# A two-layer decoder on one core: the gates' high product as scaled copies on ScalarE, late TensorE parts held behind first products, and a new schedule of gather steps

## The chip, the cores and the metric

The kernel runs on one core of one Trainium2 chip. The metric is the device time of one execution in microseconds (us). All tensors come in as float32; products of float32 matrices are made from bfloat16 halves, as told below.

## What is computed

Two layers, each a token mixer (layer 0: a gated linear recurrence beside chunked retention; layer 1: a chunked state-space mixer) and then a mixture of 16384 small experts ("PEER"), with residuals and root-mean-square norms. The change touches the expert mixer alone:

```python
q = (t @ w_q).reshape(n_tok, 8, 2, 64)
scores = einsum('thpk,hpnk->thpn', q, sub_keys)
s_top, i_top = top_k(scores, 16)
cand = s_top[:, :, 0, :, None] + s_top[:, :, 1, None, :]
best, pos = top_k(cand.reshape(n_tok, 8, 256), 16)
expert = take_along_axis(cand_idx, pos); gates = softmax(best)
u = u_emb[expert]
act = gelu(einsum('td,thkd->thk', t, u)) * gates
out = einsum('thk,thkd->td', act, v_emb[expert])
```

There are 512 tokens of width 1024, so four tiles of 128 tokens. Each token has 8 x 16 = 128 experts.

## The kernel before

**Two ways to the experts.** Tile 0 (`GT`) gathers: for its 128 tokens the kernel fetches the chosen rows of `u` and `v` by indirect DMA (`gather`, L785). Tiles 1 to 3 (`DT`, 384 tokens) are computed densely: 128 blocks of 128 experts, each with a *first product* `up(b)` (24 matmuls of 384 columns into `pu`, then a Gelu on ScalarE, L909), a multiplication with the block's gates (L1014) and a second product into six accumulators `acc` (18 matmuls of 512 columns, L82 to L84).

**Split products.** `split` (L75, L76) makes a bfloat16 high half on ScalarE and a low half on VectorE or GpSimd; `mm3` (L82 to L84) adds high x high, high x low and low x high. Weights come through `Stream`: a DMA, `whi` on ScalarE, `wlo` on GpSimd, three tiles ahead.

**The head.** After the mixer's output projection the expert part begins with a head. It routes tile 0 and then tiles 1 to 3 (`routing`: eight scores `ps`, L656, each followed by top-8 searches on VectorE; candidates; index arithmetic with the tiles `eq`, `em`, L714 to L721; then transposes into `pt`, L737 and L755). For each group of 16 tokens `gate_group` builds a dense gate table for all 16384 experts: VectorE compares the iota with the two indices (`o2`, L928; `ol`, L930), multiplies with the gate's high half (`oh`, L932) and its low half (`ol`, L933); TensorE multiplies `o2` with `oh` and `ol` per token into `pg` (L941, L942); ScalarE copies to `st` (L943), and a DMA writes `Gd`. There are 24 groups in a layer. The head is cut into 183 units (`UNITS`); `fill` puts between them first products ahead of time (`RUN[1]` = `AHEAD` + `SPILL` = 95 of 128), and `EARLY` = 100 of the 262 gather steps. First products of blocks below `SPILL` are written to DRAM (`Hd`) and read back.

**Gather steps.** One step starts one gather and uses the one of six steps before: a `u` row block is dotted with the token on VectorE (`junk`, L814), four `v` row blocks are summed in two halves of four matmuls (`av`, L839) with an addition to the residual on VectorE (L843). Steps not taken in the head are taken at the ticks of the blocks, evenly.

**The blocks.** `load_gates` reads `Gd` back (L1003) once the last group is written, and blocks 0 to 127 follow, with the remaining 33 first products between them.

**What sets the order.** The program text gives instructions their rank and buffers; a scheduler turns it into one fixed list per engine when the kernel is built. `tc.issue_after(x)` adds that an instruction stands behind `x` in its engine's list; `due` lists in `fill` say after how many units (`LATE` = 3) a transposition or a group's matmuls are put in.

## Time and profile before

| | us |
|---|---|
| median of 3 runs (lowest, highest) | 3517.67 (3515.95, 3518.49) |
| the profiled execution | 3519.76 |
| its span in the profile | 3518.0 |
| TensorE busy in the span | 3219.2 (92%) |
| VectorE busy | 2313.1 (66%) |
| GpSimd busy | 1932.0 (55%) |
| ScalarE busy | 1443.8 (41%) |

Busy is the time in which an engine has at least one instruction in work; matmuls overlap, and their ends are modelled, so a busy TensorE is not one at its peak. The profiled execution lies 2.1 us above the median, and 1.8 us of it lie outside the span. In layer 0 the head runs from 490.6 to 1042.2 us of the span and the blocks to 1733.0; in layer 1 the head runs from 2267.4 to 2821.8 and the blocks to 3510.2.

### The profile page before, as it was taken

To read this page: it belongs to the slowest core of one execution; us is meant where nothing else is said; L and a number is where in the kernel's file an instruction comes from. 1 tells how busy PE (TensorE), PEld (TensorE's weight loads), DVE (VectorE), ACT (ScalarE), POOL (GpSimd) and SP (SyncE) were. 2 spreads that over 40 slices of the span, in tenths; PEclk is the share of its full clock that TensorE was granted. 3 is DMA by queue.
4 is the path that set the end of the run, shared out by engine and by line. 5 is a ranking of instruction groups with operands and counts; after the bars stand their busy time and mean duration, and the time that the engine had idled before them with its cause. 6 is when DMAs were issued, how large, how long until landed. Compare 5 with 4: busy or idle time off the path is not lost. (4 is left out here: it accounts for less than half of the span.)

```text
span 3518.0 us, 52562 instructions
## 1 busy us (share of the span) xinstructions
PE 3219.2 (92%) x19786; PEld 1730.0 (49%) x19786; DVE 2313.1 (66%) x4286; ACT 1443.8 (41%) x2303; POOL 1932.0 (55%) x1122
## 2 busy tenths in 40 slices
PE   7999977988899999999998888788888999999999
PEld 4444554554554444444455554554545644444444
DVE  6555289977766767433567774889886677675433
ACT  5444443343443333333445555433434433333333
POOL 4444756766656665554233345577666656555552
PEclk9999999999999999999999999898999999999999
DMA  4222657797999999876321124587878999998773
GB/s 142 89 82 86 194 169 251 259 305 251 303 331 345 341 366 335 301 266 229 117 78 61 61 72 124 159 273 243 299 246 285 333 348 359 359 339 289 282 251 120
DMA packets 340672, 821.91 MB, mean 234 GB/s; under 512 B 28353, under 2 KB 179393, under 8 KB 336321
## 3 DMA queue, kind: packets, MB, share of 16 engines
q1 hardware_dynamic: 133632, 456.22, 38.0%
q0 software_dynamic: 73728, 268.47, 21.2%
q10 hardware_dynamic: 133056, 93.87, 8.3%
q8 instruction: 155, 2.54, 0.3%
q14 instruction: 101, 0.82, 0.1%
HBM read 732.98 MB, written 85.46 MB: 233 GB/s over the span
## 5 line engine op out<-in xcount | busy, mean ns | idle before, releaser
L76 POOL TENSOR_TENSOR wlo<-w,whi 128x1024 bf16<-128x1024 f32 x536 | 1199.3, 2240 | 1210.6 <-ACT whi L75 1128.3
L75 ACT ACTIVATE whi<-w 128x1024 bf16<-128x1024 f32 x696 | 730.4, 1051 | 840.2 <-PE pu L83 336.4
L82 PE MATMUL pu<-hh,whi 128*128 128x384 bf16 x2048 | 676.7, 330 | 12.3 <-ACT Hs L909 12.3
L84 PE MATMUL pu<-hh,wlo 128*128 128x384 bf16 x2048 | 675.3, 330 | 0.0
L83 PE MATMUL pu<-hl,whi 128*128 128x384 bf16 x2048 | 675.2, 330 | 0.0
L84 PE MATMUL acc<-whi,al 128*128 128x512 bf16 x1536 | 582.8, 379 | 1.4 <-DVE al L76 1.3
L82 PE MATMUL acc<-whi,ah 128*128 128x512 bf16 x1536 | 583.6, 380 | 0.0
L83 PE MATMUL acc<-wlo,ah 128*128 128x512 bf16 x1536 | 583.0, 380 | 0.0
L76 DVE TENSOR_TENSOR al<-a,ah 128x384 bf16<-128x384 f32 x256 | 154.7, 605 | 492.0 <-ACT ah L75 463.2
L814 DVE CUSTOM_DVE_ANT_0 junk<-g,hr 128x1024 bf16<-128x1024 f32 x256 | 372.2, 1454 | 89.1 <-DMA g<-u_in,ix 82.7
L82 PEld LDWEIGHTS <-whi 128*128 128x128 bf16 x2944 | 290.7, 99 | 228.7 <-issue 48.4
L83 PEld LDWEIGHTS <-whi 128*128 128x128 bf16 x2944 | 290.9, 99 | 208.7 <-issue 27.4
L84 PEld LDWEIGHTS <-wlo 128*128 128x128 bf16 x2944 | 290.7, 99 | 204.0 <-issue 21.2
L785 POOL DMA_INDIRECT g<-v_in,ix x256 | 319.4, 1248 | 126.0 <-PE av L839 68.3
L75 ACT ACTIVATE ah<-a 128x384 bf16<-128x384 f32 x256 | 133.5, 522 | 615.5 <-issue 449.9
L785 POOL DMA_INDIRECT g<-u_in,ix x256 | 323.5, 1264 | 105.7 <-issue 36.8
L82 PEld LDWEIGHTS <-ah 128*128 128x128 bf16 x1536 | 150.2, 98 | 234.7 <-issue 32.6
L84 PEld LDWEIGHTS <-al 128*128 128x128 bf16 x1536 | 150.4, 98 | 185.1 <-DVE al L76 3.1
L83 PEld LDWEIGHTS <-ah 128*128 128x128 bf16 x1536 | 150.4, 98 | 171.1 <-issue 2.4
L76 DVE TENSOR_TENSOR wlo<-w,whi 128x1024 bf16<-128x1024 f32 x160 | 195.6, 1223 | 16.8 <-ACT whi L75 15.4
L1014 DVE TENSOR_TENSOR a<-Hs,G 128x384 f32<-128x384 f32 x168 | 156.8, 935 | 68.3 <-DMA G<-Gd 46.8
L82 PE MATMUL mm<-hhi,whi 128*128 128x512 bf16 x512 | 196.2, 383 | 1.1 <-DVE cv L195 1.1
(384 smaller groups left out, 4913.1 us busy)
## 6 DMA issues: line engine op xcount, KB each, us to landing
w<-ut_in SPq DMA_DIRECT2D x256, 512.0 KB
w<-v_in SPq DMA_DIRECT2D x256, 512.0 KB
Gd<-st ACTq DMA_DIRECT2D x48, 1024.0 KB
G<-Gd SPq DMA_DIRECT2D x32, 1536.0 KB
w<-w_in SPq DMA_DIRECT2D x88, 512.0 KB
w<-wo_in SPq DMA_DIRECT2D x64, 512.0 KB
Hd<-Hs ACTq DMA_DIRECT2D x168, 192.0 KB
Hs<-Hd SPq DMA_DIRECT2D x168, 192.0 KB
```

Of the source, the lines that this page charges most:

```text
L75: nc.scalar.activation(hi, src, AF.Copy)
L76: return (lo_eng or nc.vector).tensor_tensor(lo, src, hi, op=OP.subtract)
L82: nc.tensor.matmul(out, ah, bh, start=start and i == 0, stop=False)
L83: nc.tensor.matmul(out, ah, bl, start=False, stop=False)
L84: nc.tensor.matmul(out, al, bh, start=False, stop=stop and i == n - 1)
L785: nc.gpsimd.indirect_dma_start(out=g, out_offset=None, in_=tab, in_offset=bass.IndirectOffsetOnAxis(ap=ix, axis=0))
L814: nc.vector.tensor_tensor_reduce(k.junk, g, hr, op0=OP.mult, op1=OP.add, scale=1.0, scalar=0.0, accum_out=h[:, s:s + 1])
L1014: nc.vector.tensor_tensor(a.rearrange("p (a b) -> p a b", b=GB), H[b].rearrange("p (a b) -> p a b", b=GB), g, op=OP.mult)
```

## The change

- `gate_group`: the comparison goes into a tile `om` of its own (one buffer). The high product is no longer one multiplication on VectorE but 16 copies on ScalarE, one per token, each of 128 x 128 with the token's gate as a per-partition factor (`gT`, a float32 copy of the transposed gates). The low product stays on VectorE and now reads `om`.
- `behind()`: the transposes of the routing, the groups' matmuls and the first of the four matmuls of each `av` half stand behind the last matmul of the latest first product in TensorE's list.
- `sums` calls `flush()` first, so that a second half still open is put in.
- `WAIT` = 7: gather steps, and the closing transposition of tile 0, begin after 7 units instead of 3.
- `SPILL` 84 to 90 and `AHEAD` 11 to 7: 97 instead of 95 first products in the head, 90 instead of 84 results written to DRAM and read back, 8 instead of 12 buffers for results that stay.
- `EARLY` 100 to 84: 16 gather steps move from each head into the blocks. There, a tick counts 2 below block 90 and 3 from it on (`PACES`).

```diff
-SPILL = 84
-AHEAD = 11
+SPILL = 90
+AHEAD = 7
...
-EARLY = 100
+EARLY = 84
...
+WAIT = 7
...
+PACES = 2, 3
...
+        gT = one.tile([128, TD], F32, name="gT")
...
+        latest = []
+
+        def behind():
+            return tc.issue_after(latest[-1].ins) if latest else nullcontext()
...
-            nc.tensor.transpose(pt[:, 0], e2[:, 1], k.ident)
+            with behind():
+                nc.tensor.transpose(pt[:, 0], e2[:, 1], k.ident)
...
             split(nc, pt[:, 2], ghl[:, 0, ts], ghl[:, 1, ts])
+            nc.scalar.activation(gT[:, ts], pt[:, 2], AF.Copy)
...
             def sums(i, r, h):
 
+                flush()
                 nc.scalar.activation(h, h, AF.Gelu_apprx_tanh)
...
-                            with tc.issue_after(first.ins) if first is not None else nullcontext():
+                            with tc.issue_after(first.ins) if first is not None else behind():
...
-            ticks = KEYS + KEYS - RUN[1] - SLACK
+            ticks = PACES[0] * SPILL + PACES[1] * (KEYS + KEYS - RUN[1] - SPILL - SLACK)
...
-                pace[0] += 1
+                pace[0] += PACES[at[0] >= SPILL]
...
-                mm3(nc, p, [((w[0][:, q], w[1][:, q]), (hhi[:, q], hlo[:, q])) for q in range(KD)])
+                latest.append(mm3(nc, p, [((w[0][:, q], w[1][:, q]), (hhi[:, q], hlo[:, q])) for q in range(KD)]))
...
+                om = first.tile(shape, BF, tag="om", name="om", bufs=1)
+                nc.vector.tensor_tensor(om, keys, by_token(i1T), op=OP.is_equal)
+                oh = first.tile(shape, BF, tag="oh", name="oh")
+                for t in range(GB):
+                    at = n * GB + t
+                    nc.scalar.activation(oh[:, t // 2, :, t % 2], om[:, t // 2, :, t % 2], AF.Copy,
+                                         scale=gT[:, at:at + 1])
                 ol = first.tile(shape, BF, tag="ol", name="ol")
-                nc.vector.tensor_tensor(ol, keys, by_token(i1T), op=OP.is_equal)
-                oh = first.tile(shape, BF, tag="oh", name="oh")
-                nc.vector.tensor_tensor(oh, ol, by_token(ghl[:, 0]), op=OP.mult)
-                nc.vector.tensor_tensor(ol, ol, by_token(ghl[:, 1]), op=OP.mult)
+                nc.vector.tensor_tensor(ol, om, by_token(ghl[:, 1]), op=OP.mult)
...
-                            nc.tensor.matmul(pv[:, t], o2[:, a, :, j], oh[:, a, :, j], start=True, stop=False)
+                            with behind():
+                                nc.tensor.matmul(pv[:, t], o2[:, a, :, j], oh[:, a, :, j], start=True, stop=False)
...
-                    if units[0] > LATE:
+                    if units[0] > WAIT:
...
-            due.append((LATE, lambda: next(ends, None)))
+            due.append((WAIT, lambda: next(ends, None)))
...
+                at[0] = b
                 block(b)
```

How the lists move, at three places. First, TensorE's list where the head of layer 0 begins: the first rows of the first products (`pu`, 24 matmuls each), and tile 0's closing transposition (`pt`, from VectorE's `wk`). Before:

```order
L82 MATMUL pu_4451<-hh_2723,whi_4218 128x384
...
L737 MATMUL pt_4481<-ident_64,wk_3645 128x128
L741 MATMUL pt_4481<-wk_3645,ident_64 32x32 x32
L82 MATMUL pu_4543<-hh_2723,whi_4251 128x384
...
L656 MATMUL ps_4525<-key_4523,qT_3188 128x256
```

And with the change:

```order
L667 MATMUL ps_4540<-key_4538,qT_3189 128x256
...
L86 MATMUL pu_4452<-hh_2723,whi_4219 128x384
...
L86 MATMUL pu_4504<-hh_2723,whi_4252 128x384
...
L86 MATMUL pu_4556<-hh_2723,whi_4448 128x384
...
L749 MATMUL pt_4586<-ident_64,wk_3646 128x128
L754 MATMUL pt_4586<-wk_3646,ident_64 32x32 x32
```

Three first products stand ahead of the transposition instead of one, and four scores of tile 1 (two before).

Second, TensorE's list at a pair of `av` halves while tile 3 is routed. Before, 5 matmuls of a first product stand between the halves:

```order
L839 MATMUL av_7987<-g_7571,z_6499 32x512
...
L82 MATMUL pu_8008<-hh_2723,whi_7910 128x384
...
L839 MATMUL av_7996<-g_7748,z_6499 32x512
L839 MATMUL av_7996<-g_7699,z_6499 32x512
```

With the change it is all 24:

```order
L855 MATMUL av_7912<-g_7400,z_7264 32x512
...
L86 MATMUL pu_7924<-hh_2723,whi_7818 128x384
...
L88 MATMUL pu_7924<-hh_2723,wlo_7819 128x384
L855 MATMUL av_7958<-g_7575,z_7264 32x512
```

The halves have moved apart by 19 matmuls.

Third, ScalarE's list between two groups of 16 tokens of tile 1. Before:

```order
L909 ACTIVATE Hs_8572<-pu_8547 128x384
L943 ACTIVATE st_8575<-pg_8576 128x128x4
...
L943 ACTIVATE st_8575<-pg_8606 128x128x4
L75 ACTIVATE whi_8665<-w32_8663 128x1024
L944 DMA Gd_82<-st_8575 128x16x128
L909 ACTIVATE Hs_8658<-pu_8633 128x384
```

And with the change:

```order
L926 ACTIVATE Hs_7051<-pu_7026 128x384
...
L965 ACTIVATE st_7054<-pg_7055 128x128x4
...
L951 ACTIVATE oh_7100<-om_7098,gT_2732 128x128
L966 DMA Gd_82<-st_7054 128x16x128
L951 ACTIVATE oh_7100<-om_7098,gT_2732 128x128 x15
L79 ACTIVATE whi_7124<-w32_7122 128x1024
L926 ACTIVATE Hs_7153<-pu_7128 128x384
```

The next group's 16 copies stand behind the four `st` copies of this group and ahead of the next weight's `whi`.

What stands in the lists between five marks of the head of layer 0 (layer 1 has the same counts), before / with the change. The marks are the closing transposition of tile 0 and those of tiles 1, 2 and 3, the last gate matmul, and the first block:

| TensorE's and VectorE's instructions | to tile 0 | to tile 1 | to tile 2 | to tile 3 | to last gates | to block 0 |
|---|---|---|---|---|---|---|
| `pu` matmuls | 24 / 72 | 439 / 408 | 449 / 456 | 720 / 744 | 532 / 554 | 116 / 94 |
| `pg` matmuls | 0 / 0 | 0 / 0 | 0 / 0 | 256 / 256 | 512 / 512 | 0 / 0 |
| `ps` scores | 0 / 0 | 8 / 6 | 6 / 6 | 8 / 8 | 0 / 0 | 0 / 0 |
| `av` halves | 0 / 0 | 0 / 0 | 0 / 0 | 8 / 6 | 6 / 4 | 1 / 0 |
| `junk` dots | 0 / 0 | 17 / 9 | 15 / 20 | 20 / 17 | 12 / 10 | 0 / 0 |
| `oh` products on VectorE | 0 / 0 | 0 / 0 | 2 / 0 | 8 / 0 | 14 / 0 | 0 / 0 |
| `oh` copies on ScalarE | 0 / 0 | 0 / 0 | 0 / 32 | 0 / 128 | 0 / 224 | 0 / 0 |

## Rows read from the trace of the kernel before

**Rows 1.** Busy time by stretch: heads of layers 0 and 1, blocks of layer 0
```profile
core 0: us, PE busy (x) PEld busy (x) DVE busy (x) ACT busy (x) POOL busy (x), PEclk, DMA share, GB/s
490.60:1042.20 551.60, 467.08 (x3328) 283.98 (x3325) 456.49 (x983) 207.63 (x337) 360.59 (x198) 0.94 0.82 276
2267.40:2821.80 554.40, 471.21 (x3329) 286.16 (x3327) 454.01 (x983) 207.92 (x337) 362.41 (x198) 0.93 0.82 276
1042.20:1733.00 690.80, 687.85 (x3551) 307.87 (x3547) 379.91 (x527) 247.51 (x340) 363.31 (x237) 1.00 0.82 296
```

**Rows 2.** The same view, layer 0's head cut at the five marks
```profile
490.60:507.90 17.30, 4.07 (x26) 2.25 (x23) 17.30 (x25) 4.22 (x6) 5.98 (x3) 0.75 0.38 122
507.90:604.50 96.60, 80.86 (x536) 47.78 (x536) 84.88 (x259) 32.25 (x50) 67.47 (x41) 0.92 0.79 263
604.50:698.50 94.00, 84.61 (x480) 48.92 (x481) 93.35 (x288) 32.39 (x51) 64.24 (x35) 0.92 0.74 245
698.50:879.40 180.90, 150.17 (x1070) 90.76 (x1069) 144.69 (x328) 66.10 (x106) 119.20 (x68) 0.94 0.82 276
879.40:1022.30 142.90, 127.47 (x1097) 82.88 (x1096) 113.75 (x82) 65.57 (x113) 96.42 (x50) 0.96 0.95 319
1022.30:1042.20 19.90, 19.90 (x127) 11.39 (x124) 2.52 (x5) 7.10 (x12) 7.28 (x4) 1.00 0.92 323
```

**Rows 3.** TensorE's waits, 490 to 1042 us: total us, times, longest
```profile
PE av L839 <- DVE x L843: 27.3, 5, 13.1
PE pt L755 <- DVE e L751: 14.2, 1, 14.2
PE pt L737 <- DVE wk L721: 13.2, 1, 13.2
PE pg L942 <- DVE ol L933: 8.3, 6, 2.6
...
PE pu L82 <- ACT Hs L909: 6.2, 2, 5.7
```

**Rows 4.** Busy time by stretch of tiles pu, acc and av alone
```profile
1022.30:1041.30 19.00, 18.99 (x116) 1.91 (x4) 1.00 0.92 317
1183.90:1217.20 33.30, 31.44 (x146) 0.00 (x0) 1.00 0.88 313
1183.90:1217.20 33.30, 2.13 (x16) 0.32 (x16) 1.36 (x2) 1.00 0.88 313
```

**Rows 5.** VectorE's groups by form, 490 to 1042 us: busy us, mean ns
```profile
L814 DVE CUSTOM_DVE_ANT_0 junk<-g,hr 128x1024 bf16<-128x1024 f32 x64 | 101.3, 1583 | 39.1 <-DMA g<-u_in,ix 38.7
...
L932 DVE TENSOR_TENSOR oh<-ol,ghl 128x2048 bf16<-128x2048 bf16 x24 | 36.9, 1537 | 0.6
```

**Rows 6.** ScalarE's groups by form, the whole span
```profile
L943 ACT ACTIVATE st<-pg 128x512 f32<-128x512 f32 x192 | 102.6, 600 | 45.9 <-PE pg L942 43.2 <-DMA Gd<-st 1.5 <-ACT st L943 0.2
...
L451 ACT ACTIVATE m<-pq,na 128x128 f32<-128x128 f32 x128 | 37.6, 373 | 7.3 <-DVE ml L76 5.7 <-PE pq L446 1.6
...
L75 ACT ACTIVATE mh<-m 128x512 bf16<-128x512 f32 x32 | 20.2, 632 | 11.5 <-DVE m L453 7.8 <-DVE ds L483 3.7
```

**Rows 7.** ScalarE's timeline in layer 1's mixer: start, us, instructions
```profile
1834.93 1.16 ACT L451 ACTIVATE m<-pq,na 128x128 f32<-128x128 f32 x4
```

**Rows 8.** VectorE's waits, 485 to 1040 us
```profile
DVE junk L814 <- DMA g<-u_in,ix: 38.7, 14, 12.3
DVE a L1014 <- DMA G<-Gd: 23.4, 1, 23.4
```

**Rows 9.** TensorE's timeline at a pair of av halves
```profile
839.07 1.07 PE L839 MATMUL av<-g,z 128*32 128x512 f32 x8
...
854.17 1.93 PE L839 MATMUL av<-g,z 128*32 128x512 f32 x8 [13.11 <-DVE x L843]
```

More of the change, by code (lines that the diff above doesn't have):

```diff
@@ L83, in mm3 @@
         nc.tensor.matmul(out, ah, bl, start=False, stop=False)
-        nc.tensor.matmul(out, al, bh, start=False, stop=stop and i == n - 1)
+        last = nc.tensor.matmul(out, al, bh, start=False, stop=stop and i == n - 1)
+    return last
 class Stream:
@@ L736, in routing @@
                 pt = pr.tile([128, 3, 128], F32, tag="r", name="pt")
-                nc.tensor.transpose(pt[:, 2], eff, k.ident)
+                with behind():
+                    nc.tensor.transpose(pt[:, 2], eff, k.ident)
                 for r in range(PARTS):
@@ L740, in routing @@
                         for m, src in enumerate((eff, gtf)):
-                            nc.tensor.matmul(pt[32 * q:32 * q + 32, m, r * 32:(r + 1) * 32], part(r),
-                                             src[:, 32 * q:32 * q + 32], start=True, stop=True)
+                            with behind():
+                                nc.tensor.matmul(pt[32 * q:32 * q + 32, m, r * 32:(r + 1) * 32], part(r),
+                                                 src[:, 32 * q:32 * q + 32], start=True, stop=True)
                 nc.vector.tensor_copy(idx[i], pt[:, 0:3:2])
@@ L754, in routing @@
             pt = pr.tile([128, 4, 128], F32, tag="r", name="pt")
-            nc.tensor.transpose(pt[:, 0], e2[:, 1], k.ident)
-            nc.tensor.transpose(pt[:, 1], e2[:, 0], k.ident)
-            nc.tensor.transpose(pt[:, 2], gtf, k.ident)
+            with behind():
+                nc.tensor.transpose(pt[:, 0], e2[:, 1], k.ident)
+                nc.tensor.transpose(pt[:, 1], e2[:, 0], k.ident)
+                nc.tensor.transpose(pt[:, 2], gtf, k.ident)
             nc.scalar.activation(i1T[:, ts], pt[:, 0], AF.Copy)
@@ L883, in layer @@
             steps = gathered()
-            ticks = KEYS + KEYS - RUN[1] - SLACK
+            ticks = PACES[0] * SPILL + PACES[1] * (KEYS + KEYS - RUN[1] - SPILL - SLACK)
+            at = [0]
             pace, taken = [0], [0]
@@ L940, in multiply @@
                             a, j = divmod(c + t, 2)
-                            nc.tensor.matmul(pv[:, t], o2[:, a, :, j], oh[:, a, :, j], start=True, stop=False)
-                            nc.tensor.matmul(pv[:, t], o2[:, a, :, j], ol[:, a, :, j], start=False, stop=True)
+                            with behind():
+                                nc.tensor.matmul(pv[:, t], o2[:, a, :, j], oh[:, a, :, j], start=True, stop=False)
+                                nc.tensor.matmul(pv[:, t], o2[:, a, :, j], ol[:, a, :, j], start=False, stop=True)
                         nc.scalar.activation(st[:, :, c:c + 4], pv.rearrange("p t k -> p k t"), AF.Copy)
@@ L956, in fill @@
                     units[0] += 1
-                    if units[0] > LATE:
-                        take((units[0] - LATE) * EARLY // (UNITS - LATE) - (units[0] - 1 - LATE) * EARLY // (UNITS - LATE))
+                    if units[0] > WAIT:
+                        take((units[0] - WAIT) * EARLY // (UNITS - WAIT) - (units[0] - 1 - WAIT) * EARLY // (UNITS - WAIT))
                     for j in itertools.islice(ups, share_of(RUN[1] - REST)):
```

## The prediction

> **What bounds the kernel now.** I read the busy time by stretch first, then TensorE's waits, then the prices. A layer has two parts that the change touches. In the blocks TensorE is busy 687.85 of 690.80 us at full clock [rows 1]: they cost what their matmuls cost, and one block's 18 second products take 31.44 / 8 = 3.9 us [rows 4]. In the head no engine is full on the average: TensorE 467.08 and VectorE 456.49 of 551.60 us [rows 1]. Cut at its marks, the head shows why [rows 2]. Up to tile 0's closing transposition VectorE is busy all 17.30 us and TensorE 4.07. While tiles 1 and 2 are routed, VectorE has 84.88 of 96.60 and 93.35 of 94.00. While the gates are built it is the other way round: TensorE 150.17 of 180.90 and 127.47 of 142.90. So the two engines take turns in waiting, since each has its own fixed list. TensorE's longest waits name the places [rows 3]: 13.2 us once for tile 0's indices, 14.2 us once for tile 1's, and 27.3 us in five waits of an `av` matmul for an addition on VectorE. Of the last, one of 13.11 us stands between the two halves of a pair, whose first half ended at about 840 us [rows 9]. The clock row agrees: 0.75 and 0.92 in the early stretches, 1.00 where nothing waits [rows 2]; a waiting TensorE falls from 2.4 to 1.2 GHz for a time.
>
> **Prices.** A first product's matmul takes 18.99 / 116 = 0.164 us, an `av` half 2.13 / 2 = 1.07 us [rows 4]. On VectorE a dot takes 1.58 us and an `oh` product 1.54 us [rows 5]. A scaled copy of 128 columns from SBUF by ScalarE does not occur. The nearest row is `m`, 128 columns with a per-partition factor, but from PSUM: 373 ns alone [rows 6], and four in a row take 1.16 us, so one follows the other after (1.16 - 0.373) / 3 = 0.26 us [rows 7]. SBUF instead of PSUM costs 632 - 600 = 32 ns at 512 columns [rows 6]. I take 0.29 us; the ends are 0.25 and, with no overlap at all, 0.41 us.
>
> **The change, stretch by stretch** (counts from the table of the lists, times of layer 0 from [rows 2]).
>
> To tile 0's mark, 17.3 us: VectorE's chain sets it and its rows ahead of the result are the same, so it stays 17.3. TensorE does 72 first-product matmuls in it instead of 24, 11.8 us instead of 3.9, that it would have had to do later.
>
> To tile 1's mark, 96.6 us: TensorE loses 31 matmuls, 80.9 - 5.1 = 75.8; VectorE loses 8 dots, 84.9 - 12.6 = 72.3. Both are now ready at about the same time, and the wait of 14.2 us goes. I take 78.
>
> To tile 2's mark, 94.0 us: a loss. VectorE, already full, gets 5 dots (7.9) and one comparison that moves here (1.5), and is rid of two `oh` products (3.1): 99.7. TensorE's 84.6 are hidden behind that. I take 100.
>
> To tile 3's mark, 180.9 us: TensorE gets 24 matmuls (3.9) and the 8 matmuls that spread the token rows (2.1, as two `av` halves of the same form), and is rid of two halves (2.1): 154.1. VectorE falls to 144.7 - 8 x 1.54 - 3 x 1.58 = 127.6. ScalarE rises to 66.1 + 128 x 0.29 = 103.2. TensorE sets the pace, and a whole first product (24 x 0.164 = 3.9 us) now stands between two halves, in which VectorE can add. Of the 30.7 us idle I leave a quarter: 162.
>
> To the last gates, 142.9 us: TensorE 127.5 + 22 x 0.164 - 2 x 1.07 = 129.0; VectorE 113.8 - 14 x 1.54 - 2 x 1.58 = 89.1; ScalarE 65.6 + 224 x 0.29 = 130.6. ScalarE becomes as full as TensorE, and its list is strict: 16 copies (4.7 us) behind one group's `st` and ahead of the next `whi`. With 4 us for waits between the two: 135.
>
> To block 0, 19.9 us: the products that cover the way of the last gates through DRAM shrink to 94 x 0.164 = 15.4. VectorE's wait for that way, 23.4 us [rows 8], now ends under cover. It may show by up to the present 19.9. I take 17.
>
> The head: 17.3 + 78 + 100 + 162 + 135 + 17 = 509, from 551.6, so -42.3. Layer 1's head has the same counts and takes 554.4 [rows 1]; I give it the same gain.
>
> The blocks: two first products fewer (-7.9) and five `av` halves more (+5.4), -2.5 a layer. The dots that move with them lie beside TensorE, as VectorE has 379.91 of 690.80 busy. Sixteen more gathers and six more results read back go to queues with a DMA share of 0.82 [rows 1]; the pace of 2 and 3 moves gathers from blocks with no first product to blocks with one, where a block lasts longer. In the stretch with the densest matmul rows shown a share of 0.88 left TensorE's rows close to each other [rows 4]. I cost these at nothing; if the cover were gone, it would show as a period above 3.9 us a block.
>
> Sum: 2 x (42.3 + 2.5) = 90 off the profiled execution's 3519.8, 3430. That execution lies 2.1 us above the median, less than the rounding here: **3430 us**.
>
> **Rules weighed.** In the 14 groups of the late gate stretch the copies take 4.7 us of ScalarE for 1.54 us of VectorE saved [rows 5 to 7]. The Trainium skill ("ScalarE: Activation LUTs", section "Rules for kernel authors") says to keep multiplications on VectorE, up to about three times as fast in bf16; no row here runs the same form on both, and by the rule taken alone the gate stretches would become ScalarE's: the first rival. The head's clock share of 0.94 [rows 1] means 66 us of 552 at the lower level, part of it idle. If half of that was work, 66 / 4 = 16 us a layer would come back with the waits; I leave it to the low end, 3398. The Trainium skill ("TensorE: Matmul & The Clock Gate", section "Why this matters for your kernels") would count on it, since idle gaps between bursts of matmuls are what throttles the clock.
>
> **Rivals.**
> (a) *ScalarE paces the gates.* If copies do not overlap, 0.41 us each, ScalarE has 65.6 + 224 x 0.41 = 157 in the late stretch, 160 with waits, and the eight groups before tile 3's mark take 15 more, some 170 with the rest hidden. A layer's head is 542, and all comes to 3494. For it: ScalarE's strict list, and the single `om` buffer, so that VectorE cannot compare ahead of the copies. Against: four scaled activations in a row do overlap [rows 7].
> (b) *Gathers come late.* Second halves held behind a whole product free their row buffers later. VectorE already waits 38.7 us for gathered rows [rows 8]. If both gate stretches stay at 180.9 and 142.9, the head is 536 and the sum 3519.8 - 2 x (15.5 + 2.5) = 3484. Against: six and four halves instead of eight and six, and fewer gathers in the head.
> (c) *Slower: copies block ScalarE's list.* The first groups' copies stand in that list among scores and Gelus while VectorE is full with routing. If ScalarE reaches them before `om` is compared, no weight, Gelu or score passes; TensorE stops when its three `pu` buffers are full, and then VectorE lacks scores. The nearest row is TensorE's wait for a Gelu, 5.7 us at the longest [rows 3]. It decides from 44.8 / 24 = 1.9 us a group on; at 3 us, 72 a layer, the kernel comes to 3574. Against: the copies of only two groups stand there, the others follow their comparison closely.
> (d) *The waits only move.* TensorE's list does more ahead of each transposition, but VectorE's chain ends no earlier: 3518. Against: VectorE's head loses some 50 us of work by the counts above (24 x 1.54 + 8 x 1.58 = 49.6).
>
> **How the numbers follow.** My forecast 0.60, (a) 0.15, (b) 0.13, (c) 0.09, (d) 0.03. About 0.2% (7 us) is what a measurement of this kernel can tell from no change; the sum, (a) and (b) lie beyond it. Faster by more 0.87, within it 0.04, slower 0.09. With copies at 0.25 us and no waits left the stretches give 17.3 + 75.8 + 99.7 + 154.1 + 129.0 + 15.4 = 491, a sum of 3394; the clock's 16 us would go further, but not in full on top. Range 3390 to 3495, which takes in (a) and (b) and leaves out (c), (d) and a little on either end.
>
> **What would show it.** Right: TensorE's wait for tile 1's transposition under 3 us, and its longest `av` wait below 10; tile 2's stretch a few us longer than before, with the wait for its transposition grown to over 10 us; 768 copies a pass at 0.25 to 0.3 us from start to start; ScalarE above 85% in the late gate stretch; heads of 495 to 525 us; blocks at 3.9 us plus 1.07 a half. Wrong: copies that follow each other after 0.4 us (a), VectorE's wait for gathers above 60 us a head (b), ScalarE idle for VectorE's `om` by tens of us while TensorE waits for Gelus (c), or a head of 550 us with the transposition waits still there (d).

## The result and the profile after

The change makes the kernel slower: 3611.77 us median of 4 runs (3609.09 to 3623.28) against 3518.08 (3515.95 to 3520.74), a ratio of 1.0272, 95% interval 1.0249 to 1.0295. The prediction was 3430 us in a range of 3390 to 3495, with a chance of 0.09 for slower. The profiled execution took 3623.28 us, 103.5 us more than that of before; it lies 11.5 us above its median, so the stretches below add up to somewhat more than the medians' difference.

Busy time by stretch in the changed kernel, layer 0, cut at the marks of [rows 2]; the first row lies ahead of the head, the last is the blocks:

```profile
core 0: us, PE busy (x) PEld busy (x) DVE busy (x) ACT busy (x) POOL busy (x), PEclk, DMA share, GB/s
0.00:499.80 499.80, 449.74 (x2599) 251.21 (x2633) 265.71 (x518) 242.72 (x347) 253.41 (x139) 0.98 0.39 123
499.80:512.80 13.00, 13.00 (x74) 7.52 (x72) 13.00 (x45) 3.25 (x6) 4.16 (x2) 0.90 0.16 52
512.80:593.90 81.10, 74.62 (x502) 43.42 (x500) 72.52 (x221) 31.95 (x49) 57.81 (x33) 0.98 0.78 253
593.90:708.20 114.30, 84.46 (x473) 49.55 (x473) 97.77 (x290) 42.84 (x84) 66.72 (x41) 0.87 0.64 221
708.20:894.70 186.50, 161.21 (x1093) 95.09 (x1092) 134.10 (x307) 106.56 (x239) 113.08 (x62) 0.92 0.78 258
894.70:1067.50 172.80, 140.92 (x1102) 89.39 (x1100) 81.70 (x62) 129.41 (x335) 78.83 (x44) 0.91 0.79 245
1067.50:1086.40 18.90, 15.62 (x97) 9.24 (x96) 1.43 (x3) 7.65 (x13) 9.34 (x5) 0.99 0.92 334
1086.40:1789.10 702.70, 681.74 (x3468) 304.03 (x3536) 406.49 (x550) 248.57 (x341) 396.67 (x253) 1.00 0.84 306
```

Set against [rows 1, 2], this shows where the 56 us of this layer come from: 9.2 ahead of the head, 35.0 in the head, 11.9 in the blocks. In the head, tile 1's stretch is 15.5 us shorter; tile 2's is 20.3 longer, tile 3's 5.6, and the late gates' 29.9. In that last stretch ScalarE does 129 us of work, where 131 were forecast, but no engine is full: TensorE is busy 141 of 173 us, and its clock share is 0.91 instead of 0.96. Layer 1 repeats it, more weakly in the head (577.1 us against 554.4; blocks 702.6 against 688.5).

TensorE's waits in the head, 490 to 1087 us: total us, times, longest.

```profile
PE av L855 <- DVE x L859: 24.9, 4, 10.2
PE pu L88 <- POOL wlo L80: 20.5, 15, 2.0
PE pu L86 <- ACT Hs L926: 16.6, 2, 9.3
PE ps L667 <- ACT gT L775: 13.2, 1, 13.2
PE ps L667 <- ACT sc L669: 8.5, 2, 6.7
PE pu L86 <- ACT whi L79: 7.9, 6, 1.8
```

Both waits for transpositions of [rows 3] are gone. But there are new ones for the weights' halves (`wlo`, `whi`), of which the same view of before has none, and longer ones of the score products (`ps`; 3.9 us before) and for Gelus. Only the wait for the additions kept its place.

The scaled copies, in the page's list of groups and in ScalarE's timeline of one round of the late stretch (start, us, instructions, idle time before them and what ended it):

```profile
L951 ACT ACTIVATE oh<-om,gT 128x128 bf16<-128x128 bf16 x768 | 239.8, 425 | 47.1 <-DVE om L947 39.7
```

```profile
1005.66 4.53 ACT L951 ACTIVATE oh<-om,gT 128x128 bf16<-128x128 bf16 x15
1010.06 1.04 ACT L79 ACTIVATE whi<-w 128x1024 bf16<-128x1024 f32 x1
1011.01 0.47 ACT L926 ACTIVATE Hs<-pu 128x384 f32<-128x384 f32 x1
1011.38 1.04 ACT L79 ACTIVATE whi<-w 128x1024 bf16<-128x1024 f32 x1
...
1012.70 0.58 ACT L965 ACTIVATE st<-pg 128x512 f32<-128x512 f32 x1
...
1017.31 0.60 ACT L965 ACTIVATE st<-pg 128x512 f32<-128x512 f32 x1 [3.02 <-PE pg L964]
1017.80 0.43 ACT L951 ACTIVATE oh<-om,gT 128x128 bf16<-128x128 bf16 x1
```

TensorE's rows with a wait in the same round:

```profile
1011.16 0.34 PE L86 MATMUL pu<-hh,whi 128*128 128x384 bf16 x1 [1.80 <-ACT whi L79]
1013.49 0.34 PE L88 MATMUL pu<-hh,wlo 128*128 128x384 bf16 x1 [1.83 <-POOL wlo L80]
```

A copy follows a copy after (4.53 - 0.43) / 14 = 0.29 us, as forecast. But the two engines take turns: TensorE waits until ScalarE, through with 16 copies, splits the next weight, and then for GpSimd's half of it; it thereby comes late with the gate products, and now ScalarE waits 3 us for those. Over the whole stretch the two directions read:

```profile
PE pu L88 <- POOL wlo L80: 13.8, 10, 1.8
PE av L855 <- DVE x L859: 8.9, 1, 8.9
PE pu L86 <- ACT whi L79: 6.1, 5, 1.8
```

```profile
ACT st L965 <- PE pg L964: 30.4, 13, 7.8
ACT oh L951 <- DVE om L947: 6.6, 3, 2.8
ACT gT L775 <- DVE ghl L80: 4.4, 1, 4.4
```

### The profile page after: what moved, and what is told of

Read it like the earlier page. It is cut to its first block, busy times and chain, and to the rows that moved or that the text cites. A ratio compares the mean times of both kernels' runs of the same rounds, so it can differ in the third digit from the quotient of the medians.

```text
span 3621.5 us, 53161 instructions
## 1 busy us (share of the span) xinstructions
PE 3254.4 (90%) x19574; PEld 1742.5 (48%) x19786; DVE 2255.9 (62%) x4236; ACT 1677.4 (46%) x3080; POOL 1937.7 (54%) x1124
## 3 DMA queue, kind: packets, MB, share of 16 engines
q0 software_dynamic: 73728, 268.47, 20.7%
## 5 line engine op out<-in xcount | busy, mean ns | idle before, releaser
L86 PE MATMUL pu<-hh,whi 128*128 128x384 bf16 x2048 | 689.5, 337 | 58.5 <-ACT Hs L926 34.1
L88 PE MATMUL pu<-hh,wlo 128*128 128x384 bf16 x2048 | 688.9, 336 | 39.8 <-POOL wlo L80 39.8
L87 PE MATMUL pu<-hl,whi 128*128 128x384 bf16 x2048 | 688.2, 336 | 0.0
L87 PE MATMUL acc<-wlo,ah 128*128 128x512 bf16 x1506 | 572.5, 380 | 14.2 <-ACT ah L79 5.2
L88 PE MATMUL acc<-whi,al 128*128 128x512 bf16 x1496 | 568.3, 380 | 3.3 <-DVE al L80 1.7
L86 PE MATMUL acc<-whi,ah 128*128 128x512 bf16 x1468 | 557.5, 380 | 2.7 <-issue 0.3
L829 DVE CUSTOM_DVE_ANT_0 junk<-g,hr 128x1024 bf16<-128x1024 f32 x256 | 396.6, 1549 | 186.3 <-DMA g<-u_in,ix 174.4
L80 DVE TENSOR_TENSOR al<-a,ah 128x384 bf16<-128x384 f32 x256 | 165.8, 648 | 382.5 <-ACT ah L79 382.2
L951 ACT ACTIVATE oh<-om,gT 128x128 bf16<-128x128 bf16 x768 | 239.8, 425 | 47.1 <-DVE om L947 39.7
L855 PE MATMUL av<-g,z 128*32 128x512 f32 x1024 | 141.6, 626 | 59.8 <-DVE x L859 59.8
```

What stands on the lines that cost most here:

```text
L80: return (lo_eng or nc.vector).tensor_tensor(lo, src, hi, op=OP.subtract)
L86: nc.tensor.matmul(out, ah, bh, start=start and i == 0, stop=False)
L87: nc.tensor.matmul(out, ah, bl, start=False, stop=False)
L88: last = nc.tensor.matmul(out, al, bh, start=False, stop=stop and i == n - 1)
L829: nc.vector.tensor_tensor_reduce(k.junk, g, hr, op0=OP.mult, op1=OP.add, scale=1.0, scalar=0.0, accum_out=h[:, s:s + 1])
L855: m = nc.tensor.matmul(av[32 * j:32 * j + 32, :], z[:, j, a * 32:a * 32 + 32], rows[j][:, c * 512:(c + 1) * 512], start=True, stop=True)
```

## The experiments

Times are medians; the kernel before, measured beside the runs, took 3516.2 to 3517.5. The ratios are to these; they are not quotients of the medians, and differ from those by up to 0.001. "Late" is the stretch from tile 3's mark to the last gate product in layer 0, with ScalarE's and TensorE's busy time and the clock share in it.

| run | us | ratio to before (95%) | late | ScalarE | TensorE | clock |
|---|---|---|---|---|---|---|
| before | 3518.08 | | 142.9 | 65.6 | 127.5 | 0.96 |
| the change | 3611.77 | 1.0272 (1.0249 to 1.0295) | 172.8 | 129.4 | 140.9 | 0.91 |
| e1 copies undone | 3522.31 | 1.0018 (1.0005 to 1.0031) | 141.3 | 65.8 | 128.6 | 0.95 |
| e2 copies alone | 3607.51 | 1.0257 (1.0223 to 1.0291) | 167.0 | 129.3 | 142.5 | 0.93 |
| e3 holds undone | 3638.27 | 1.0353 (1.0323 to 1.0384) | 173.7 | 129.3 | 144.5 | 0.90 |
| e4 holds alone | 3519.49 | 1.0005 (0.9990 to 1.0019) | 143.4 | | | |
| e5 copies spread | 3614.38 | 1.0276 (1.0255 to 1.0298) | 172.1 | 131.5 | 143.0 | 0.92 |
| e6 half the copies | 3551.42 | 1.0093 (1.0071 to 1.0115) | 144.3 | 98.2 | 128.3 | 0.99 |
| e7 old blocks, no copies | 3505.94 | 0.9973 (0.9955 to 0.9992) | 141.0 | 65.6 | 128.7 | 0.95 |
| e8 spill alone | 3528.51 | 1.0034 (1.0018 to 1.0050) | 141.9 | 65.7 | 127.7 | 0.96 |
| e9 gate copies on VectorE | 3602.56 | 1.0248 (1.0232 to 1.0263) | 167.5 | 96.7 | 148.8 | 0.89 |
| e10 two compare buffers | 3585.44 | 1.0200 (1.0184 to 1.0216) | 165.5 | 129.1 | 138.0 | 0.93 |
| e11 numbers alone | 3506.68 | 0.9969 (0.9956 to 0.9981) | 142.7 | | | |
| e12 wait of five | 3497.09 | 0.9945 (0.9932 to 0.9959) | 140.2 | | | |
| e13 weight ahead of copies | 3624.92 | 1.0298 (1.0271 to 1.0324) | 171.7 | 130.3 | 143.8 | 0.90 |
| e14 both loosened | 3625.52 | 1.0312 (1.0289 to 1.0336) | 177.9 | 130.1 | 146.8 | 0.88 |
| e15 wait alone | 3505.20 | 0.9968 (0.9954 to 0.9982) | 138.0 | 65.5 | 124.9 | 1.00 |
| e16 gate products later | 3598.37 | 1.0237 (1.0211 to 1.0262) | 165.8 | 128.6 | 136.4 | 0.97 |
| e17 copies nobody reads | 3603.34 | 1.0244 (1.0223 to 1.0265) | 171.6 | 127.9 | 142.3 | 0.89 |
| e18 later products, no copies | 3498.83 | 0.9944 (0.9925 to 0.9963) | 145.0 | 65.0 | 127.1 | 0.95 |

### Which part of the change costs

The theory after the first look: the copies (S). The rivals: the holds (H), the schedule numbers (N). Taking the copies out, and putting them in alone:

```diff
-                om = first.tile(shape, BF, tag="om", name="om", bufs=1)
...
-                for t in range(GB):
...
-                    nc.scalar.activation(oh[...], om[...], AF.Copy, scale=gT[:, at:at + 1])
...
+                nc.vector.tensor_tensor(oh, ol, by_token(ghl[:, 0]), op=OP.mult)
...
```

> The changed kernel with the high product back on VectorE (om, gT and the 768 scaled copies gone), holds, schedule numbers and spill as changed. Theory S (the copies fill ScalarE's strict list, weights' halves wait behind them and TensorE behind those): the stretch from tile 3's mark to the last gates falls from 172.8 to about 140 us, tile 2's from 114 to about 103, tile 3's from 186 to about 170, both layers alike, and the kernel takes about 3500 us (3480 to 3530). Theory H (the holds behind whole first products keep second halves, and with them row buffers and gathers, late): the copies were cover, VectorE gets 24 products of 1.5 us more a layer, and it stays at 3600 or above. Theory N (the schedule numbers: scores ahead of tile 0's end, more steps in the blocks): 3590 to 3610.

> The kernel before with the scaled copies on ScalarE, and with 90 products spilled and 7 ahead, without which om and gT find no room in SBUF; no holds, no new pace, the old numbers for the gather steps in the head. Theory S: the late gate stretch grows from 142.9 to 165 us or more, the kernel to 3570 to 3620. Theories H and N: copies relieve VectorE, 3490 to 3525.

The ground for the copies alone is the spill alone (`SPILL` 90, `AHEAD` 7 in the kernel before):

> The kernel before with 90 products spilled and 7 ahead, nothing else: the ground on which the copies alone stand. In the run of the copies alone the blocks took 685 us, 5 less than before, for two first products fewer. The head gets those two products (7.8 us a layer): 3510 to 3520 if they lie in its waits or not. Theories S and P say that the copies alone, 3607.5, lose 85 to 100 us against this; if this itself takes 3560 or more, part of that was the spill's.

With the copies undone the kernel is back at 3522.3; alone they cost 3607.5 - 3528.5 = 79 us, in the change 3611.8 - 3522.3 = 90. S holds. The spill alone, 12 us slower than before, is outside the range given for it. In the run with the copies undone the stretches of layer 0 from tile 2's mark on and the blocks are these:

```profile
701.80:875.90 174.10, 156.04 (x1093) 93.03 (x1092) 133.22 (x315) 68.22 (x110) 115.35 (x63) 0.95 0.83 279
875.90:1017.20 141.30, 128.58 (x1080) 85.10 (x1078) 102.67 (x77) 65.78 (x112) 84.55 (x46) 0.95 0.94 307
1017.20:1036.10 18.90, 18.90 (x121) 11.44 (x119) 2.17 (x4) 6.71 (x12) 7.67 (x4) 1.00 0.89 324
1036.10:1735.90 699.80, 688.39 (x3539) 304.52 (x3537) 402.91 (x549) 247.62 (x339) 393.34 (x252) 0.99 0.84 306
```

The late stretch gives back 31.5 us of the copies' price in this layer, tile 3's 12.4 (25.4 and 14.4 in layer 1).

The holds, by making `behind()` return a null context, and by adding them alone (with the `flush()` in `sums`):

```diff
         def behind():
-            return tc.issue_after(latest[-1].ins) if latest else nullcontext()
+            return nullcontext()
```

> The changed kernel with every hold behind the latest first product taken out; copies, numbers and spill as changed. Theory H: second halves and transpositions go early again, the waits for gathered rows fall, and it comes to 3540 or less. Theory S: it stays at 3590 to 3630, since ScalarE's list is the same. Theory N: 3600.

> The kernel before with the holds alone (and the second half before a new part's sums): the old products on VectorE, the old numbers and spill. Theory H: 3560 or more. Theory S: no copies, so the head keeps its stretches but the waits for the transpositions of tiles 0 and 1 go: 3480 to 3515. Theory N: 3510 to 3520.

H falls: the holds alone change nothing, and under the copies they save 3638.3 - 3611.8 = 26.5 us. Theory S had 3590 to 3630 for their removal, so this much is unexplained. S was also wrong on the holds alone, for which it had 3480 to 3515: with them the stretches of tiles 0 and 1 are 16.6 and 96.2 us long, as before, so the holds are not what took the transposition waits away. The numbers are:

```diff
-EARLY = 100
+EARLY = 84
...
+WAIT = 7
```

> The kernel before with the head's numbers alone (84 gather steps in place of 100, first step and tile 0's end after 7 units in place of 3): no holds, no copies, old spill and pace. Holds alone did nothing (3519.5), holds with these numbers gave 3505.9. If the numbers alone make that gain, 3502 to 3510; if they need the holds, 3514 to 3530.

> The changed kernel without the copies and with the old spill and pace in the blocks (84 products spilled, 11 ahead, one pace): holds and the head's numbers (84 gather steps, wait of 7 units) remain. With copies undone the heads took 12 us a layer less than before, but the blocks 9 more and the work ahead of the head 6 more. If the blocks' loss came from spill and pace, 3500 (3495 to 3510); if from the 16 gather steps that the head leaves to the blocks, 3518 to 3525 as with copies undone.

With the numbers alone the stretches of tiles 0 and 1 take 12.8 and 81.4 us. They make the kernel 0.3% faster than before, with or without the holds. Spill and pace cost the rest of that gain: 3522.3 - 3505.9 = 16 us, which is why the kernel with the copies undone is no faster than the one before.

### How the copies cost

First, the copies' place in the list (P) against their volume (V). A group's 16 copies were spread over three units, and separately the first half of them went back to VectorE:

```diff
-                for t in range(GB):
...
-                    nc.scalar.activation(...)
...
+                scaled(0, 6)
+                due.append((units[0] + 1, lambda: scaled(6, 11)))
+                due.append((units[0] + 2, lambda: scaled(11, 16)))
```

> The changed kernel with the same 768 scaled copies, but a group's 16 copies stand in ScalarE's list as 6, 5 and 5, a unit of routing or filling apart, so that weights' halves, Gelus and the gate copies stand between them (most of them now as runs of 6, 10, 11 and 5). Theory P (place: the run of 16 copies between one group's gate copies and the next weight's first half makes TensorE wait, and TensorE's late gate products make ScalarE wait in turn): the late gate stretch falls from 172.8 to 150 us or less, the kernel to 3540 to 3575. Theory V (volume: ScalarE at 129 us of work has no room in that stretch, wherever its copies stand): 3595 to 3620.

```diff
+                nc.vector.tensor_tensor(oh[:, :GB // 4], om[:, :GB // 4], ..., op=OP.mult)
-                for t in range(GB):
+                for t in range(GB // 2, GB):
```

> The changed kernel with the high product of a group's first 8 tokens back on VectorE in one instruction (half as large), 8 copies on ScalarE: 384 copies a pass. Theory V: half of the loss, 3560 to 3570, ScalarE's work in the late stretch about 98 us. Theory P: the run between the gate copies and the next weight falls from 4.7 to 2.4 us, below the slack of three weights ready ahead, and most of the loss goes: 3530 to 3545.

Spread, they cost the same; halved, two thirds of the 90 us go (60), and the late stretch is within 3 us of that without copies, at nearly full clock:

```profile
877.90:1022.20 144.30, 128.30 (x1103) 84.63 (x1102) 95.89 (x76) 98.15 (x223) 79.94 (x44) 0.99 0.91 292
```

So it isn't the run of 16 in one place, as far as the spreading goes (most of the pieces still held 5 to 11 copies). The halving fell between the ranges of P and V. Then three ties between ScalarE's list and others were loosened, one by one: the gate copies `st` on VectorE, two buffers for `om`, and the next weight split ahead of the copies.

```diff
-                        nc.scalar.activation(st[:, :, c:c + 4], pv.rearrange("p t k -> p k t"), AF.Copy)
+                        nc.vector.tensor_copy(st[:, :, c:c + 4], pv.rearrange("p t k -> p k t"))
```

> The changed kernel with all 768 scaled copies on ScalarE, but the 192 copies of the gate products from PSUM (st, 0.5 us each from start to start) on VectorE. ScalarE's work in the late gate stretch falls from 129 to about 101 us, VectorE's rises from 82 to some 118. Theory V (volume: ScalarE, with 129 of 141 us, cannot run the two weights ahead that hide GpSimd's second half and TensorE's late products): as with half the copies, late stretch 144 us, 3540 to 3560. If it is the scaled copies' own order against the compare (om) that counts, and not ScalarE's volume, it stays at 3600 or above; if VectorE then waits for TensorE in ScalarE's place, 3575 to 3600.

```diff
-SPILL = 90
-AHEAD = 7
+SPILL = 93
+AHEAD = 4
...
-                om = first.tile(shape, BF, tag="om", name="om", bufs=1)
+                om = first.tile(shape, BF, tag="om", name="om", bufs=2)
```

> The changed kernel with two buffers for om instead of one, and to make room 93 products spilled and 4 ahead. VectorE waited 86 us a pass for om until the copies were through, ScalarE only 40 us for om. Theory V: VectorE's waits for om go, ScalarE's work is the same: 3590 to 3625. If the single buffer ties the two engines' lists together (the other reading of those waits), the late stretch falls to 155 or less and the kernel below 3575.

```diff
+                while len(k.W.ready) < k.W.ahead and k.W.drams:
+                    k.W.emit()
                 for t in range(GB):
```

> The changed kernel, but in each gate group the next weight is split ahead of the group's 16 scaled copies instead of behind them; the copies, their number and everything else stay. Theory L (loop: a group's gate copies wait for TensorE's gate products, the next group's scaled copies stand behind them, the next weight's first half behind those, GpSimd's second half and TensorE's products behind that, and the next gate products behind those; so 4.7 us of copies lie in the round): the copies fall out of the round, the late gate stretch goes from 172.8 to 155 us or less, the kernel to 3560 to 3585. If the room on ScalarE alone counts (129 us of work), it stays at 3600 or above.

> The weight ahead of the copies and two buffers for om (93 products spilled, 4 ahead, as in the run with two buffers, 3585.4). Theory L: both ties are loosened, the late stretch comes to 145 to 150 us, the kernel to 3535 to 3565. If room on ScalarE alone counts, 3580 to 3590 as with two buffers.

None brings the stretch back. With `st` on VectorE, ScalarE has no more work than with half the copies (96.7 us), yet the stretch stays at 167.5 us. The wait has moved with `st`: VectorE now waits for the gate products, and ScalarE for VectorE. V had 3540 to 3560 for this run, so ScalarE's room alone is not the whole of it.

```profile
ACT oh L951 <- DVE o L945: 26.2, 3, 11.9
ACT oh L951 <- issue: 21.1, 3, 9.7
ACT oh L951 <- DVE st L965: 13.9, 3, 7.1
```

```profile
DVE st L965 <- PE pg L964: 45.2, 28, 8.0
```

The weight ahead of the copies (theory L) made it no faster (13 us slower, which the two intervals hardly tell apart), so L falls. The second buffer gave 26 us, too little for the tie and too much for V, and nothing together with that weight; its part in the late stretch is 7 us, and why the rest came is open, since the scheduler drew up all lists anew. Last, the lock step itself (theory R), and volume without any use:

```diff
-                due.append((units[0] + LATE, multiply))
+                due.append((units[0] + 5, multiply))
```

> The changed kernel with a group's gate products put in 5 units after its compares in place of 3, so that they and their gate copies come after the next group's scaled copies. Theory R (round in lock step: the gate products of a group wait for its own 16 copies, its gate copies stand just ahead of the next group's 16 copies, and ScalarE and TensorE take turns): with a group's copies a whole step ahead of their use the turns overlap, the late stretch falls from 172.8 to 155 us or less, the kernel to 3560 to 3590. Theory V (ScalarE's room alone): 3600 to 3625.

```diff
+                no = first.tile([128, KEYS], BF, tag="no", name="no", bufs=2)
+                for t in range(GB):
+                    at = n * GB + t
+                    nc.scalar.activation(no, o2[:, t // 2, :, t % 2], AF.Copy, scale=gT[:, at:at + 1])
```

> The kernel with the copies undone (3522.3: the high product on VectorE), and on top of it 16 scaled copies a group on ScalarE into a tile that nobody reads: the same number, size and factor, with o2 as their source. ScalarE has the same 129 us of work in the late stretch, but no gate product waits for a copy, and the lists may hold them later. Theory V: 3590 or more. Theory R: the copies lie beside the other work, 3525 to 3550.

With copies that nobody reads, added where the copies were undone, the kernel loses 3603.3 - 3522.3 = 81 us, nearly the whole price, and the late stretch looks as in the change:

```profile
879.10:1050.70 171.60, 142.30 (x1103) 89.05 (x1102) 95.54 (x77) 127.90 (x325) 78.34 (x44) 0.89 0.79 252
```

VectorE waits no more than 3.8 us for these copies there. So it is neither the gate products' need of the copies nor their buffer that costs most of the time, but the copies' being in ScalarE's list at all, read or not. The other instructions are not slower beside them: in the late stretch a `wlo` takes 2.27 us on the average in the change and 2.24 with the copies undone, a `whi` 1.04 and 1.06, so the price is paid in waits. Theory R explains at most the 13 us that the later gate products gave, which the two intervals hardly tell apart either: the wait for `pg` fell from 30.4 to 13.3 us, but TensorE's waits for the weights' halves stayed (20.6 us, 19.9 in the change), and ScalarE still idled 37 us.

### What beats both kernels

The edits to the changed kernel, beside the copies undone (e7 keeps a wait of 7, e15 has `EARLY` = 100, e18 the later gate products of e16):

```diff
-SPILL = 90
-AHEAD = 7
+SPILL = 84
+AHEAD = 11
...
-WAIT = 7
+WAIT = 5
...
-PACES = 2, 3
+PACES = 1, 1
```

> Holds and 84 gather steps without copies and with the old blocks, as in the run that took 3505.9, but tile 0's end and the first gather step after 5 units in place of 7. With 7, two score products stood ahead of the head and cost it 5 to 7 us a layer, and tile 2's mark came 10 us later. With 5 the scores may stay behind tile 0's end: 3495 to 3505 if that loss goes and the wait for tile 1's transposition stays away; 3510 or more if that wait (14 us) comes back.

> The kernel of 3497.1 (holds, 84 gather steps, wait of 5 units, old blocks, no copies) with 100 gather steps in the head again. The blocks take back 5 second halves a layer (699 to some 692 us each). If the head's gain came from the wait, the heads stay at 535 us and the kernel comes to 3480 to 3490; if it came from fewer gather steps, the heads go back to 545 to 550 and it takes 3505 to 3518.

> The fastest kernel so far (3497.1: holds, 84 gather steps, wait of 5, old blocks, no copies) with the gate products put in after 5 units in place of 3. Its late stretch takes 140 us with 128 us of TensorE's work in it; if TensorE's waits for oh and ol (13 us a layer) go: 3480 to 3492; if the later products only shift the waits to o2's buffers: 3495 to 3505.

Holds, 84 gather steps, a wait of 5 units, old spill and pace, and no copies: 3497.1 us, 0.55% less than before. In its profiled execution (3486.8 us, the fastest of its runs) the heads take 535.0 and 526.5 us, 17 and 28 less than [rows 1]. Both numbers have a share: with 100 steps the heads take 544.8 and 543.7, and the blocks 12 and 8 us less. Later gate products add nothing here.

## Why the prediction failed

Layer 0, stretch by stretch (us). The prediction gave no time for the way to the head; 490.6 is what its sum takes over unchanged.

| | before | forecast | changed | copies undone |
|---|---|---|---|---|
| ahead of the head | 490.6 | 490.6 | 499.8 | 496.7 |
| to tile 0 | 17.3 | 17.3 | 13.0 | 12.7 |
| to tile 1 | 96.6 | 78 | 81.1 | 82.9 |
| to tile 2 | 94.0 | 100 | 114.3 | 109.5 |
| to tile 3 | 180.9 | 162 | 186.5 | 174.1 |
| to the last gates | 142.9 | 135 | 172.8 | 141.3 |
| to block 0 | 19.9 | 17 | 18.9 | 18.9 |
| blocks | 690.8 | 688.3 | 702.7 | 699.8 |

The change missed the forecast of this layer by 101 us: 37.8 in the late stretch, 24.5 in tile 3's, 14.4 in the blocks, 14.3 in tile 2's, 9.2 ahead of the head.

**The step that failed: "With 4 us for waits between the two: 135."** The prices under it were right: 0.29 us a copy, and ScalarE's work in the late stretch 129.4 us against 130.6. The term for waits was mis-sized by ten: ScalarE idles 172.8 - 129.4 = 43 us. In the eight other runs of the table with 16 copies a group and the gate copies on ScalarE it idles 36 to 48 us, wherever the copies stand and whoever reads them. In these runs the stretch's length is ScalarE's work plus some 40 us of taking turns. With half the copies it idles 46 us, and the stretch (144.3 us) is little longer than without any, with TensorE's work of 128 us in it; between 98 and 129 us of ScalarE's work no run was made. With the gate copies on VectorE the sum does not hold (96.7 us of work in 167.5). A sum that takes the fuller of two engines and adds a little would hold if one of them could run ahead of the other; in the round shown above each waits for the other. Why it is about 40 us, whichever tie is loosened, stays open. Not tried: GpSimd's half of the weights on VectorE in this stretch.

**Rival (a) had the engine and not the mechanism.** It let ScalarE pace the gates through copies that do not overlap, 0.41 us each, a head of 542 us and 3494 in all. The copies overlap; the head took 586.6. I gave it 0.15 and let it end below the old time: with [rows 2] at hand, TensorE idling 15 of 143 us beside a half-empty ScalarE, a ScalarE as full as TensorE should have been the slower rival. Rival (c), the one that was slower, had ScalarE's strict list holding back the weights, but at another place and for another reason: the copies of the first groups, among the routing, cost 4.8 us (114.3 against 109.5 to tile 2's mark), and ScalarE's waits for `om` are 18.9 and 20.7 us a head, 6.6 of them in the late stretch of layer 0, where it waits 30.4 us for gate products. TensorE's waits for Gelus, named with them as (c)'s sign, are 16.6 and 17.5 us a head, but 13.7 and 12.7 without copies. The sign of (b), more than 60 us a head of VectorE's waiting for gathered rows, came true in layer 0. Its lines in the changed kernel's head and in that with the copies undone:

```profile
DVE junk L829 <- DMA g<-u_in,ix: 61.9, 17, 12.8
```

```profile
DVE junk L827 <- DMA g<-u_in,ix: 40.7, 13, 12.4
```

So the wait goes with the copies and not with the held halves, and (b) was not the cause: with the copies undone and the gathers as changed, the kernel is within 0.2% of its old time.

**The clock.** The late stretch has a clock share of 0.91 with the copies, 0.95 without, 0.99 with half of them. For the same matmuls TensorE is busy 140.9 us with the copies and 128.3 with half of them. In the trace 31 us of the stretch lie at 1.2 instead of 2.4 GHz, and TensorE is busy in 23 of them; with half of the copies it is 3 us. Half of the difference, some 10 of the 28.5 us between these two stretches, is what the clock took. It is not what makes the stretch long: with the later gate products (e16) the share is 0.97, and the stretch takes 165.8 us. The prediction counted on a gain of the clock for the low end; it went the other way. The Trainium skill ("TensorE: Matmul & The Clock Gate", section "Why this matters for your kernels") makes idle gaps between bursts the cause of a throttled clock. The trace agrees in that the falls stand behind waits; the sum of the idle time does not tell them (in this stretch TensorE idles 29 us in e16 at a share of 0.97, and 32 in the change at 0.91).

**The rule against the change.** One `oh` product of 16 tokens takes VectorE 1.49 us in the run with the copies undone (20.9 us for 14); the 16 copies that replace it take 16 x 0.29 = 4.7. The Trainium skill ("ScalarE: Activation LUTs", section "Rules for kernel authors") says to leave multiplications to VectorE, up to about three times as fast in bf16, a figure for operations with a single source. The ratio here is 3.1, but of one two-source instruction against 16 copies. I made the rule a rival and did not follow it; in the late stretch VectorE was busy 114 of 143 us and did not set the pace, as e1 shows, where TensorE has 128.6 of 141.3, so there was little to win by relieving it.

**Tile 0: moved rows that I did not count.** I wrote that VectorE's chain sets tile 0's mark and that its rows ahead of it are the same. But two score products of tile 1 now stand ahead of the first product, where no stretch of mine began, and wait there for a score tile that VectorE has to free:

```profile
498.82 1.22 PE L667 MATMUL ps<-key,qT 128*128 128x256 f32 x2 [6.66 <-ACT sc L669]
```

```profile
498.38 0.38 ACT L669 ACTIVATE sc<-ps 128x256 f32<-128x256 f32 x1 [6.97 <-DVE sc L675]
509.77 0.39 ACT L669 ACTIVATE sc<-ps 128x256 f32<-128x256 f32 x1 [9.72 <-DVE sc L675]
```

The mark comes 4.9 us later than before (512.8 against 507.9), though VectorE has tile 0's last index at 508.3, only 0.4 later than before (the first row below is the changed kernel's, the second that of before):

```profile
506.72 1.58 DVE L732 TENSOR_REDUCE wk<-em 128x16 f32<-128x800 f32 x1
```

```profile
506.30 1.56 DVE L721 TENSOR_REDUCE wk<-em 128x16 f32<-128x800 f32 x1
```

It is now TensorE's list that sets the mark: the three first products ahead of the transposition stand behind those scores and take the 13.0 us up to it. With a wait of 5 units instead of 7 the scores stay behind, and the first product starts at 487.3. In all 13 traces with the wait of 7 it starts at 492.5 to 499.8 us, in the seven with 3 or 5 at 483.8 to 490.7.

**Tile 1: right.** 81.1 us for 78 forecast, the wait for its transposition gone. It was the numbers that took it away (81.4 with them alone), not the holds, which change nothing alone. **Tile 2: the loss was seen, its size not.** VectorE has the work that I counted (97.8 us for 99.7) but is not full: scores come late behind it, and ScalarE waits 18.0 us, once, for a part's dots (`hk`), with Gelus and weights behind it; TensorE then waits for Gelus. Without copies that wait is the same (17.6 us), so 9.5 of the 14.3 us beyond my 100 come from the rest of the change. **Tile 3:** the changed kernel's 186.5 are 12.4 of copies above the 174.1 without them; the 12 us between these and my 162 are not explained. The run with a wait of 5 and no copies reaches 162.1, but that is no confirmation: its tiles 1 and 2 take longer, and from tile 0's mark to tile 3's it needs the same 356 us as e7 with its wait of 7.

**Blocks: costed at -2.5, measured +11.9.** The five second halves cost about what I said, or somewhat more: with the old spill and pace the blocks of the two layers take 5.9 and 7.7 us more in e7, and 7 to 10 in e11 and e12, for 5.4 forecast. The two first products fewer did not show: with the spill alone the blocks are 0.8 and 1.1 us shorter, not 7.9. "I cost these at nothing" was the wrong step for fewer buffers and a quicker pace, by what is left over; no run has the pace alone. TensorE, which had hardly a wait there, has some (layer 0's blocks, changed kernel):

```profile
PE av L855 <- DVE x L859: 8.3, 6, 3.1
PE pu L86 <- ACT H L926: 4.9, 3, 3.5
PE acc L87 <- ACT ah L79: 2.6, 1, 2.6
```

Of what would show it right, the wait for tile 1's transposition and the copies' pace came true. TensorE's longest `av` wait, 10.2 us, just missed its 10; tile 2's stretch grew by 20 us instead of a few, and without the wait for its transposition that was to show; ScalarE above 85% (it is 75%), heads of 495 to 525 us and blocks at their old price did not come.

## What to carry to other kernels

Where two engines hand work to each other within fixed lists in every group, do not size a stretch by the fuller one: take the waits of both from the trace, and expect that the second engine is full well below 100%: here it was at 75%. Before moving work to the less busy engine, add as much work that nobody reads to its list: that prices the move without the rest of the change. Test the parts of a change one at a time: this one held a gain of 0.3%, of its gather numbers, beside a loss of 2.5%.

## What the runs showed of the hardware

One and the same form on VectorE, the low product `ol` of 128 x 2048, took 1.22 us or about 3 us. In the changed kernel 20 of the 48 took about 3 us, and all of these overlap a GpSimd second half; the 17 that overlap none are all short. VectorE's and GpSimd's timelines of the round shown above:

```profile
1005.23 1.23 DVE L954 TENSOR_TENSOR ol<-om,ghl 128x2048 bf16<-128x2048 bf16 x1
...
1011.48 3.03 DVE L954 TENSOR_TENSOR ol<-om,ghl 128x2048 bf16<-128x2048 bf16 x1
```

```profile
1011.18 2.25 POOL L80 TENSOR_TENSOR wlo<-w,whi 128x1024 bf16<-128x1024 f32 x1 [6.90 <-ACT whi L79]
```

The collisions moved with the change and did not grow: the 14 low products of the late stretch took 2.26 us on the average in the changed kernel and 1.74 without the copies, but the comparisons took less (1.37 us against 1.63 for the one, 1.25 against 1.47 for the other). VectorE's work in that stretch fell from 102.7 to 81.7 us, by the whole 20.9 us of the high products.
